# Sample states of a four-head recurrence made one head later, the last ones behind the next block's norm

## The chip, the cores and the metric

One core of a Trainium2 chip runs the whole program. The metric is the device time in microseconds (us) of one execution; the kernel before was timed three times. A profile is one further execution. The engines are TensorE (PE, matmuls; PEld its weight loads), VectorE (DVE), ScalarE (ACT), GpSimd (POOL) and SyncE (SP), which only issues DMAs here.

## The reference, cut to what matters

One decoder layer works on 2048 prompt tokens behind 16 learned meta tokens, and on 8 separate sample tokens that have states of their own. The part that the change touches is a gated recurrence with 4 heads and a 128x128 state for each head:

```python
f = lb + (1.0 - lb) * sigmoid(f_logit);  k = 1.0 - f
S_t = diag(f_t) S_{t-1} + k_t v_t^T       # one state per head; the prompt from zero, each sample from its own
o_t = S_t^T q_t
o = rms_norm_per_head(o) * norm_g * silu(g)
```

For the prompt this is computed in chunks of 64 tokens. A sample has a single step: read its state, multiply it by f, add the outer product of k and v, write it out (8 samples x 4 heads x 64 KB), and multiply it by q. A diagonal state-space mixer (S5), an output projection, a second RMSNorm and a gated convolutional FFN complete the layer.

## The kernel before

The prompt goes through in four blocks of 512 tokens (b = 0 to 3). Block 0 carries the 16 meta tokens and the 8 samples as 24 more columns. Every fp32 operand of a large matmul is split into two parts by ACT (`wh`, `ah`) and DVE (`wl`, `al`), and each product is made of three matmuls.

For each block the code first makes the normalised, transposed input (`norm1(b)`, through `norm_block`: L538 loads 128 rows, L530 squares them, L520 and L521 make the factor, L542 scales, L547 transposes, L86 multiplies by the gain, L552 and L83 split), then runs `head(b, a, h)` for the four heads, and then `u_proj(b, a)`, the input of the S5 mixer (matmuls L480, evictions L778). In block 0 the code of `s5_factors`, `s5_setup` and `s5_rotations` stands among this: it makes S5's tables and stores them in DRAM (`tab_d`).

In block 0, `head` has two parts. The prompt part makes f, k, the running products and q (L610 to L646), v and g (L500, L514), the chunk states and outputs (L690 to L714), the norm (L720 to L723) and the transposed result `mixh` (L726, L732). The sample part (L735 to L767) does, in this order: transpose k of the samples (L736, L738), spread v (L741), load the 8 states (L745) and multiply them by f on POOL (L746), make the outer products on PE (L749) and add them (L80), store the states (L751), make the meta tokens' scores (L753), multiply by q (L757, L758), normalise (L760 to L763) and write 10 columns of `mixh` (L765 to L767). It reads the prompt part's tiles `kd` (of `hk`) and `qd` (of `hP`), which have two buffers each, in L753.

Buffers set much of the order. The pool `x4p` has two buffers: each sample part takes both (`vb` for the spread v, `s0` for the states), and the row tiles of `norm1` take the same two. PSUM has three banks `mm` for the large matmuls, three banks `hg` for the heads, two banks `tp`. The scratch pool `nt` has four buffers, used by `norm_block` (`tm`) and by `u_proj` (`us`).

The order of instructions in each engine's queue is made by the framework's scheduler: what stands earlier in the code has priority, and later instructions fill in where the scheduler expects an engine to be free. Each queue then runs in its order. So table work of `s5_rotations` (L413 to L442) stands between instructions of heads 2 and 3 in the queues, though its code comes behind all four heads.

Of the kernel before, what the change touches and what calls it, by code (L numbers as in the profile page):

```python
# [9 lines left out]
F32 = mybir.dt.float32  # L10
# [12 lines left out]
W = META + BT + NS  # L23
PW = W
MT, SP = BT, BT + META
# [12 lines left out]
def kernel(  # L38
# [7 lines left out]
    nc = tc.nc  # L46
# [6 lines left out]
    sm = pool("sm", 4)  # L53
# [10 lines left out]
    exa = pha.enter_context(tc.tile_pool(name="exa", bufs=1))  # L64
# [29 lines left out]
    def gbank():  # L94
        return pg.tile([128, 512], F32, name="hg")
# [173 lines left out]
    E = {}  # L269
# [134 lines left out]
    def s5_rotations():  # L404

        rt = u_tile()
        mc, ms = v3(rt, 7, 32), v3(rt[:, 224:], 7, 32)
        t0, t1 = rt[:, 448:480], rt[:, 480:512]
        nc.vector.tensor_copy(mc[:, 0], sv[:, C4])
        nc.vector.tensor_copy(ms[:, 0], sv[:, S4])  # L410
        for i in range(1, 7):
            c, s_ = mc[:, i - 1], ms[:, i - 1]
            stt(ms[:, i], s_, 2.0, c, op0=OP.mult, op1=OP.mult)  # L413
            mul(t0, s_, s_)
            ts_(mc[:, i], t0, -2.0, 1.0, op0=OP.mult, op1=OP.add)
            unit(mc[:, i], ms[:, i], t0, t1)
        for q in range(4):
            tab = bigt()
            X, Y = v3(tab, 8, 129), v3(tab[:, 1032:], 8, 129)
            gs = slice(8 * q, 8 * q + 8)  # L420

            def mate(lo, n):
                ACT(Y[0:64, :, lo:lo + n], X[64:128, :, lo:lo + n], AF.Copy, scale=-1.0)
                ACT(Y[64:128, :, lo:lo + n], X[0:64, :, lo:lo + n], AF.Copy)

            nc.gpsimd.memset(X[0:64, :, 0:1], 1.0)
            nc.gpsimd.memset(X[64:128, :, 0:1], 0.0)
            nc.vector.tensor_copy(X[0:64, :, 1], sv[0:64, C4, gs])
            ts_(X[64:128, :, 1], sv[64:128, S4, gs], -1.0, None, op0=OP.mult)
            mate(0, 2)  # L430
            ta = rt[:, 512 + 512 * (q % 2):1024 + 512 * (q % 2)]
            for i in range(7):
                n = 1 << i
                tav = v3(ta, 8, n)
                X1 = X[:, :, n + 1:2 * n + 1]
                mul(X1, X[:, :, 1:n + 1], mc[:, i, gs, None].to_broadcast([128, 8, n]))
                mul(tav, Y[:, :, 1:n + 1], ms[:, i, gs, None].to_broadcast([128, 8, n]))
                sub(X1, X1, tav)
                mate(n + 1, n)
            for src, lo, hi in ((X, TC, TS), (Y, TS, TC)):  # L440
                for p, o in ((slice(0, 64), lo), (slice(64, 128), hi)):
                    dma(tab_d[2 * q:2 * q + 2, p].rearrange("b p x -> p b x")[:, :, o:o + 516],  # L442
                        src[p].rearrange("p (b g) j -> p b (g j)", b=2))
# [156 lines left out]


    def head(b, a, h):
        S = S_st[:, h, :]
        c0, c1 = 0, W if b == 0 else BT
        cols = ((0, 256), (256, W - 256)) if b == 0 else ((0, BT),)
# [28 lines left out]
        pq = fm_mm(wq, a, 8, cols)  # L634
# [3 lines left out]
        if b == 0:  # L638
            ksm = sm.tile([128, 8], F32, name="ksm", bufs=2)
            nc.vector.tensor_copy(ksm, kk[:, SP:W])  # L640
            qmd = E["qm"].rearrange("p a b -> p (a b)")[:, 32:32 + 41 * 7 + 1:41]
            nc.vector.tensor_copy(qmd, pq[1][0][:, SP - 256:W - 256])
        kd = kk
        mul(kd[:, c0:c1], ks, R[:, c0:c1])
        lead = lambda t: t[:, 0:BT].rearrange("p (c h s) -> p c h s", h=2, s=64)[:, :, 0, :]
# [17 lines left out]
        for t2_ in range(2):  # L663
            p = v3(bank(), 2, 256)
# [7 lines left out]
        if b == 0:  # L672
            pe = bank()
            ex_mm(pe[:, :256], wu, (4, 4), E["stat"], 104)
            t = ex_sum(pe, 40, 64, 256)
            ie = exa.tile([40, 256], F32, name="ie")
            add(ie, pe[:40, :256], t)
            ge = exa.tile([40, 128], F32, name="ge")
            ACT(ge, ie[:, 128:256], AF.Silu)

            nc.vector.tensor_scalar(kt[:, MT:SP], kd[:, MT:SP], pl[:, 8:9], None, op0=OP.mult)
            pm = gbank()
            nc.tensor.transpose(pm[:16, :128], kt[:, MT:SP], ident)
            ktm = exa.tile([16, 128], F32, name="ktm")
            nc.vector.tensor_copy(ktm, pm[:16, :128])
# [41 lines left out]
        if b % 2:  # L727
            mh = E["mxp"].tile([128, BT], F32, name="mixh", bufs=4)
        else:
            mh = hgp.tile([128, 10 + BT], F32, name="mixh", bufs=4)  # L730
        ng = vec[:, NG + h:NG + h + 1]
        ACT(mh[:, :BT], px.rearrange("p a b -> p (a b)"), AF.Copy, scale=ng)  # L732
        if b == 0:

            tp = gbank()  # L735
            nc.tensor.transpose(tp[:8, :128], ksm, ident)  # L736
            kts = exa.tile([40, 128], F32, name="kts")
            ACT(kts[32:40], tp[:8, :128], AF.Copy)  # L738
            vb = x4()
            vbd = v3(vb, 8, 128)[32:40]  # L740
            tt_(vbd, ie[32:40, None, 0:128].to_broadcast([8, 8, 128]),  # L741
                                    ident[32:40, 32:40, None].to_broadcast([8, 8, 128]), op=OP.mult)
            s0 = x4()
            s0v = v3(s0, 8, 128)
            dma_w(s0v, state_hgrn[0, :, h].rearrange("n k v -> k n v"))  # L745
            nc.gpsimd.tensor_tensor(s0v, s0v, fsm[:, :, None].to_broadcast([128, 8, 128]), op=OP.mult)  # L746
            for i in range(2):
                p = gbank()
                mm(p, kts[32:40], vb[32:40, 512 * i:512 * i + 512], start=True, stop=True)  # L749
                add(s0[:, 512 * i:512 * i + 512], s0[:, 512 * i:512 * i + 512], p)  # L750
            dma(hg_s[0, :, h].rearrange("n k v -> k n v"), s0v)  # L751
            pa = gbank()
            mm(pa[:16, :16], kd[:, MT:SP], qd[:, MT:SP], start=True, stop=True)  # L753
            nc.vector.copy_predicated(E["atte"][:, 0:16], mask[:16, :16], pa[:16, :16])
            po = gbank()
            for n in range(8):
                mm(po[:40, :128], E["qm"][:, n, :], s0v[:, n, :], start=(n == 0), stop=False)  # L757
            mm(po[:40, :128], E["atte"], ie[0:16, 0:128], start=False, stop=True)  # L758
            ss = sm.tile([128, 1], F32, name="ss", bufs=6)
            ACT(junk[:40, :128], po[:40, :128], AF.Square, accum_out=ss[:40])  # L760
            r = rstd_of(ss[:40], 1, 1.0 / 128)
            me = exa.tile([40, 128], F32, name="me")
            stt(me, po[:40, :128], r, ge, op0=OP.mult, op1=OP.mult)  # L763
            pm = gbank()
            nc.tensor.transpose(pm[:, :40], me, ident[:40, :40])  # L765
            ts_(mh[:, FM_:FS], pm[:, 14:16], ng, None, op0=OP.mult)
            ts_(mh[:, FS:FS + 8], pm[:, 32:40], ng, None, op0=OP.mult)  # L767
        return mh

    def u_proj(b, a):  # L770

# [237 lines left out]
    def norm1(b):  # L1009
        A[b] = new_act(b)  # L1010
        if b == 0:
            norm_block(None, NMIX, A[b], range(0, 2), x_first)
            ex_in(A[b])
            norm_block(None, NMIX, A[b], range(2, 4), x_first)
        else:
            norm_block(lambda t: x_prompt[0, b * BT + t * 128:b * BT + t * 128 + 128, :], NMIX, A[b])
# [7 lines left out]
    for b in range(NB):  # L1024
        MIX[b] = []
        last = b == NB - 1
        if b > 0:
            M[b - 1] = new_act(b - 1)
        for h in range(4):
            if last and h == 2:  # L1030
                U[b] = u_proj(b, A[b])
                fin = []
                stage_out(b - 1, lambda q: s5(b, U[b], None, (q,), fin))
                M[b] = new_act(b)
                for f in fin:
                    f(M[b])
            if last and h < 2:
                s5(b - 1, U[b - 1], M[b - 1], range(4 * h, 4 * h + 4))
            elif last:
                s5(b, U[b], M[b], (2 * h, 2 * h + 1))  # L1040
            elif b > 0:
                s5(b - 1, U[b - 1], M[b - 1], (2 * h, 2 * h + 1))
            MIX[b].append(head(b, A[b], h))
            if b == 0 and h == 0:
                s5_factors()
                setup = s5_setup()
                next(setup)
            if b == 0 and h == 1:
                next(setup, None)
        if last:  # L1050
            break
        if b == 0:
            s5_rotations()
            norm1(1)
        U[b] = u_proj(b, A[b])
        if b == 0:
            pha.close()
            E["mxp"] = pool1("mxp", 4)
        else:
            glu(b - 1, M[b - 1])  # L1060
            norm1(b + 1)
            mix_split(b - 1, M[b - 1], MIX[b - 1])
            out_proj(b - 1, M[b - 1])
# [221 lines left out]
```

## Time and profile before

| | us |
|---|---|
| timed runs: median (lowest, highest) | 2586.27 (2585.12, 2598.17) |
| profiled execution, its own time | 2598.71 |
| its span on the core | 2597.0 |
| PE busy in the span | 2475.8 (95%) |
| DVE busy | 1453.3 (56%) |
| ACT busy | 903.6 (35%) |
| POOL busy | 167.9 (6%) |

The profiled execution took 12.44 us (0.48%) more than the median of the timed ones. Busy time counts instructions, weight loads of PE apart; POOL's spans are rough. PEclk is the granted share of TensorE's full clock: 1.00 is 2.4 GHz and 0.5 is 1.2 GHz. A wait in brackets behind an instruction is the idle time of its engine before it and what ended it.

### The profile page before, as it was taken

Reading aid. Unit: us, or ns where it says so; the run is one execution under the profiler, and the core shown is the slowest. Engines: PE = TensorE matmul, PEld = TensorE weight load, DVE = VectorE, ACT = ScalarE, POOL = GpSimd, SP = SyncE. Lnnn points to the kernel's source line nnn. Section 1 sums busy time; section 2 is a strip of 40 time slices with the busy share of each in tenths; the row PEclk is TensorE's granted clock in tenths of the full one; section 3 lists DMA queues with packets and bytes.
Section 4 is the critical chain, followed back from the end, with each engine's and each line's share of the span. In section 5 each row is a group of like instructions: output and inputs, shape, how many; then the busy total and the mean of one; then the engine's idle time right before and its main releaser. Section 6 shows DMA issues by size and latency. Waiting matters only on the chain.

```text
span 2597.0 us, 35488 instructions
## 1 busy us (share of the span) xinstructions
PE 2475.8 (95%) x14315; PEld 2149.5 (83%) x14315; DVE 1453.3 (56%) x2954; ACT 903.6 (35%) x1552; POOL 167.9 (6%) x254
## 2 busy tenths in 40 slices
PE   7896998999998999999999999999999999999998
PEld 6785876898887888898988888889888888888886
DVE  6875688668668688564343433344843333333444
ACT  3544354434434445342322222223531313131222
POOL 2232100100000000100000000000310000000000
PEclk9897999999999999999999999999999999999999
DMA  4346433544464562642111111111441111111111
GB/s 128 101 126 190 110 104 130 140 152 139 123 189 144 160 221 88 228 124 65 49 49 44 47 49 41 49 41 50 156 130 49 49 49 49 49 49 49 41 53 77
DMA packets 263658, 252.22 MB, mean 97 GB/s; under 512 B 11367, under 2 KB 233471, under 8 KB 259390
## 3 DMA queue, kind: packets, MB, share of 16 engines
q1 hardware_dynamic: 253416, 220.42, 28.1%
q0 software_dynamic: 9904, 29.48, 3.5%
q8 instruction: 112, 1.84, 0.3%
q14 instruction: 52, 0.43, 0.1%
q10 hardware_dynamic: 174, 0.06, 0.0%
HBM read 216.41 MB, written 33.27 MB: 96 GB/s over the span
## 4 chain that ended last, share of the span: by engine, by line
PE 72%; DVE 10%; issue 4%; ACT 3%; DMA 3%; POOL 1%; SPq 0%; POOLq 0%; ACTq 0%; DVEq 0%
PE mm L480 42%; PE mm L1209 9%; PE hg L1209 9%; PE mm L500 7%; DVE hf L632 1%; PE mm L514 1%; DVE wl L83 1%; DVE sB L86 1%; POOL rstd L521 1%; DVE sA L885 1%; PE tp L899 1%; DMA st<-in_w_in_dram 1%; DVE sA L86 1%; PE tp L547 1%; PE tp L847 1%
## 5 line engine op out<-in xcount | busy, mean ns | idle before, releaser
L480 PE MATMUL mm<-ah,wh 128*128 128x512 f32 (+3 forms) x2320 | 819.8, 353 | 4.5 <-ACT ah L552 3.3
L480 PE MATMUL mm<-al,wh 128*128 128x512 f32 (+3 forms) x2320 | 816.6, 352 | 1.1 <-DVE al L83 1.1
L480 PE MATMUL mm<-ah,wl 128*128 128x512 f32 (+3 forms) x2320 | 816.5, 352 | 0.5 <-DVE wl L83 0.5
L449 ACT ACTIVATE wh<-st 128x1024 fp32r<-128x1024 f32 (+1 forms) x264 | 275.7, 1046 | 731.1 <-PE mm L480 317.2
L83 DVE TENSOR_TENSOR wl<-st,wh 128x1024 fp32r<-128x1024 f32 (+1 forms) x264 | 318.2, 1206 | 345.6 <-ACT wh L449 344.0
L480 PEld LDWEIGHTS mm<-ah,wh 128*128 128x128 f32 x2320 | 442.5, 191 | 60.3 <-ACT ah L552 3.9
L480 PEld LDWEIGHTS mm<-ah,wl 128*128 128x128 f32 x2320 | 442.1, 191 | 55.9 <-DVE wl L83 1.0
L480 PEld LDWEIGHTS mm<-al,wh 128*128 128x128 f32 x2320 | 442.2, 191 | 55.2 <-DVE al L83 1.6
L500 PE MATMUL mm<-wh,ah 128*128 128x256 f32 x1024 | 294.5, 289 | 8.3 <-ACT hg L671 3.2
L500 PE MATMUL mm<-wh,al 128*128 128x256 f32 x1024 | 293.5, 287 | 5.9 <-DVE al L83 5.0
L500 PE MATMUL mm<-wl,ah 128*128 128x256 f32 x1024 | 291.6, 286 | 1.1 <-DVE wl L83 1.1
L500 PEld LDWEIGHTS mm<-wh,ah 128*128 128x128 f32 x1024 | 197.5, 193 | 11.6 <-ACT hg L671 3.4
L500 PEld LDWEIGHTS mm<-wh,al 128*128 128x128 f32 x1024 | 198.0, 193 | 8.4 <-DVE al L83 6.2
L500 PEld LDWEIGHTS mm<-wl,ah 128*128 128x128 f32 x1024 | 197.5, 193 | 1.8 <-DVE wl L83 1.5
L86 DVE TENSOR_TENSOR c<-c,mm 128x512 f32<-128x512 f32 (+1 forms) x110 | 63.8, 580 | 211.8 <-PE mm L480 210.4
L1209 PE MATMUL mm<-wh,gh 128*128 128x512 f32 x352 | 137.5, 391 | 0.0
L1209 PE MATMUL hg<-wh,gl 128*128 128x512 f32 x352 | 137.2, 390 | 0.0
L1209 PE MATMUL hg<-wl,gh 128*128 128x512 f32 x352 | 137.2, 390 | 0.0
L1209 PE MATMUL mm<-wh,gl 128*128 128x512 f32 x352 | 137.2, 390 | 0.0
L1209 PE MATMUL mm<-wl,gh 128*128 128x512 f32 x352 | 137.2, 390 | 0.0
L1209 PE MATMUL hg<-wh,gh 128*128 128x512 f32 x352 | 137.1, 389 | 0.0
L80 DVE TENSOR_TENSOR hacc<-hacc,hg 128x512 f32<-128x512 f32 x96 | 65.8, 686 | 88.2 <-PE hg L1209 87.7
(384 smaller groups left out, 3050.4 us busy)
## 6 DMA issues: line engine op xcount, KB each, us to landing
st<-in_ffn_w_up_dram SPq DMA_DIRECT2D x96, 512.0 KB
big<-tab_d SPq DMA_DIRECT2D x32, 1156.0 KB
st<-in_w_in_dram SPq DMA_DIRECT2D x48, 512.0 KB
st<-in_ffn_w_down_dram SPq DMA_DIRECT2D x40, 512.0 KB
st<-in_w_in_dram SPq DMA_DIRECT2D x64, 256.0 KB
st<-in_w_out_dram SPq DMA_DIRECT2D x32, 512.0 KB
x<-in_x_prompt_dram SPq DMA_DIRECT2D x30, 512.0 KB
h_d<-x POOLq DMA_DIRECT2D x16, 512.0 KB, 5.1
```

The lines of the kernel that those rows point to most:

```text
L80: tt_(o, a, b, op=OP.add)
L83: tt_(o, a, b, op=OP.subtract)
L86: tt_(o, a, b, op=OP.mult)
L449: ACT(hi[:, :n], st[:, :n], AF.Copy)
L480: mm(p[:, :n], w[wi][:, k, :], a[ai][:, k, c0:c0 + n], start=(i == 0), stop=(i == 3 * nk - 1))
L500: o = mm(dst, lhs(ai, k), (hi, lo)[wi][:, kk, :], start=(i == 0), stop=(i == tot - 1))
L514: mm(dst[:m], stat[:, k, :m], w[:, kk, :], start=(i == 0), stop=(i == tot - 1))
L521: nc.gpsimd.tensor_tensor(r, r, mhalf[:ss.shape[0], :n], op=OP.pow)
L547: nc.tensor.transpose(p[:, k, :], x[:, kk * 128:kk * 128 + 128], ident)
L632: nc.vector.reciprocal(R[:, c0:c1], P[:, c0:c1])
L847: mm(pes[i // ng][:, i % ng, :], Bk[:, i, :], UT[:, i // 2, :nj], start=True, stop=True)
L1209: mm(ps_[t], gs[b, f0 + k][ai][:, t * 128:t * 128 + 128], wus[i][wi][:, kk, :], start=(k == 0 and j == 0), stop=(k == nf - 1 and j == 2))
```

## The change

`head` becomes a generator. In block 0 it stops behind the prompt part (`yield`); the loop then lets the sample part of the head before it run, so that in the code the order is: prompt 0, prompt 1, sample 0, prompt 2, sample 1, prompt 3, sample 2, `norm1(1)`, sample 3, `s5_rotations`, `u_proj(0)`. Before, it was prompt 0, sample 0, ..., prompt 3, sample 3, `s5_rotations`, `norm1(1)`, `u_proj(0)`. What a sample part needs later gets a place that lasts: q of the samples is copied into a small tile `qsm` and from there into `qm` when the sample part runs, and `ie` and `ge` get two buffers.

```diff
@@ head
         if b == 0:
             ksm = sm.tile([128, 8], F32, name="ksm", bufs=2)
             nc.vector.tensor_copy(ksm, kk[:, SP:W])
-            qmd = E["qm"].rearrange("p a b -> p (a b)")[:, 32:32 + 41 * 7 + 1:41]
-            nc.vector.tensor_copy(qmd, pq[1][0][:, SP - 256:W - 256])
+            qsm = sm.tile([128, 8], F32, name="qsm", bufs=2)
+            nc.vector.tensor_copy(qsm, pq[1][0][:, SP - 256:W - 256])
...
-            ie = exa.tile([40, 256], F32, name="ie")
+            ie = exa.tile([40, 256], F32, name="ie", bufs=2)
...
-            ge = exa.tile([40, 128], F32, name="ge")
+            ge = exa.tile([40, 128], F32, name="ge", bufs=2)
...
         ACT(mh[:, :BT], px.rearrange("p a b -> p (a b)"), AF.Copy, scale=ng)
-        if b == 0:
+        MIX[b].append(mh)
+        if b == 0:
+            yield
+            qmd = E["qm"].rearrange("p a b -> p (a b)")[:, 32:32 + 41 * 7 + 1:41]
+            nc.vector.tensor_copy(qmd, qsm)
             tp = gbank()
...
-        return mh
@@ the loop over the heads
-            MIX[b].append(head(b, A[b], h))
+            hd = head(b, A[b], h)
+            if b == 0:
+                next(hd)
+                if h:
+                    next(samples, None)
+                samples = hd
+            else:
+                for _ in hd:
+                    pass
...
         if b == 0:
+            norm1(1)
+            next(samples, None)
             s5_rotations()
-            norm1(1)
         U[b] = u_proj(b, A[b])
```

## Rows read from the trace of the kernel before

**Rows 1.** The page: the span, PE's busy time, the granted clock in 40 slices.

```profile
span 2597.0 us, 35488 instructions
...
PE 2475.8 (95%) x14315; PEld 2149.5 (83%) x14315; DVE 1453.3 (56%) x2954; ACT 903.6 (35%) x1552; POOL 167.9 (6%) x254
...
PEclk9897999999999999999999999999999999999999
```

**Rows 2.** Busy time by stretch: from:to, length, busy by engine, PEclk, DMA share, GB/s.

```profile
71.00:80.00 9.00, 8.55 (x42) 5.68 (x41) 5.97 (x35) 2.95 (x7) 1.62 (x2) 0.81 0.20 58
121.00:130.00 9.00, 7.78 (x38) 5.20 (x38) 8.49 (x27) 2.16 (x4) 4.40 (x7) 0.81 0.72 186
...
165.00:176.00 11.00, 11.00 (x42) 6.73 (x41) 6.72 (x16) 5.13 (x12) 2.54 (x3) 0.61 0.26 72
...
213.00:226.00 13.00, 12.03 (x54) 7.71 (x54) 7.75 (x22) 5.07 (x15) 2.96 (x5) 0.74 0.83 251
226.00:250.00 24.00, 8.55 (x36) 6.68 (x35) 13.46 (x25) 10.03 (x20) 5.45 (x10) 0.56 0.55 188
250.00:272.00 22.00, 22.00 (x147) 20.99 (x146) 5.25 (x13) 5.87 (x10) 4.34 (x8) 0.94 0.47 148
```

**Rows 3.** Waits of PE from 40 to 270 us: total, times, longest.

```profile
PE tp L547 <- DVE x L542: 7.5, 1, 7.5
PE tp L547 <- DVE rstd L520: 6.9, 1, 6.9
...
PE mm L714 <- DVE Sp L710: 1.4, 1, 1.4
```

**Rows 4.** The chain of work that ended last, from 218 us: start, us, what.

```profile
218.52 0.69 DVE x L80
...
219.78 7.42 DMA out_dram<-x
...
227.28 4.35 DMA x<-in_x_prompt_dram
...
235.72 5.89 DMA x<-in_x_prompt_dram
...
249.44 27.53 PE mm L480 x168
```

**Rows 5.** The eviction line of u_proj, 200 to 272 us: durations, first and last start.

```profile
L778 ACT ACTIVATE nt<-mm x8: 363/370/384, 249.0 to 267.0; 128x256 f32<-128x256 f32 x8
```

**Rows 6.** PE in order of time, around the sample parts of heads 1 to 3.

```profile
122.22 0.30 PE L726 MATMUL hg<-ident,hg 128*128 128x128 f32 x1 [1.27 <-DVE hg L723]
...
123.37 1.98 PE L749 MATMUL hg<-x,kts 8*128 8x512 f32 x4
125.28 0.22 PE L753 MATMUL hg<-hP,hk 128*16 128x16 f32 x2
...
126.10 3.38 PE L757 MATMUL hg<-x,qm 128*40 128x128 f32 x16
129.40 0.59 PE L758 MATMUL hg<-ie,atte 16*40 16x128 f32 x2
...
164.76 0.33 PE L726 MATMUL hg<-ident,hg 128*128 128x128 f32 x1 [1.52 <-DVE hg L723]
...
200.05 1.16 PE L701 MATMUL hg<-hv,hf 128*128 128x128 f32 x8 [3.04 <-ACT hf L698]
```

**Rows 7.** DVE in order of time: head 2 takes its k tile.

```profile
126.08 0.42 DVE L615 TENSOR_SCALAR hk<-hf 128x536 f32<-128x536 f32 x1
```

**Rows 8.** SP's queue in order of time: the state load of head 3.

```profile
198.99 0.51 SPq L745 DMA_DIRECT2D x<-in_state_hgrn_dram  x1
```

**Rows 9.** POOL and DVE in order of time: the multiplication by f, and DVE beside it.

```profile
204.37 1.95 POOL L746 TENSOR_TENSOR x<-x,fsm 128x1024 f32<-128x1024 f32 x1 [4.48 <-DMA x<-in_state_hgrn_dram]
...
204.68 2.19 DVE L83 TENSOR_TENSOR big<-big,U 128x512 f32<-128x512 f32 x1
...
226.25 0.69 DVE L83 TENSOR_TENSOR big<-big,U 128x512 f32<-128x512 f32 x1
```

## The prediction

> **What bounds the kernel now.** I read the page first: PE is busy for 95% of the span, and its granted clock is full almost everywhere except in the first slices [rows 1]. So a change pays only where PE waits or runs at a low clock, and all of this change lies in the first tenth of the span. I then cut that tenth into stretches. Two things stand out [rows 2]. From 226 to 250 us PE is busy for 8.55 of 24 us. And in the four stretches that hold the sample parts (from 71, 121, 165 and 213 us) the mean granted clock is 0.81, 0.81, 0.61 and 0.74, a mixture of the 2.4 and 1.2 GHz levels. In the third of them PE was busy without a pause, but with the sample part's small matmuls, and it had waited for head 2's own norm just before (the 1.52 us ahead of 164.76 [rows 6]).
>
> The list of PE's waits names the two large ones [rows 3]: both stand before the transposes of `norm1(1)`, 7.5 and 6.9 us. The chain of work says what they hang on [rows 4]: the last addition to head 3's new states (218.52), the store of these states (7.42 us), which must end before their buffer is free, the load of a row tile into that buffer (4.35 us), its norm, a second load (5.89 us), its norm, and only then the matmuls of `u_proj` go on at 249.44. These matmuls themselves need nothing of the norm. They stand still because their banks are not emptied: the first eviction of `u_proj` starts at 249.0 [rows 5], though the three banks were filled well before. In the code `u_proj` draws its scratch tiles behind those of `norm1(1)`, out of the same four buffers, so its evictions wait for that norm. From the last addition of head 3's sample part to the first eviction it is 249.0 − 218.5 = 30.5 us, most of it three transfers and work on one tile at a time.
>
> **The change part by part.** Nothing leaves the program. Added are four copies `qsm` to `qm` of 128x8 elements on DVE. DVE is busy for 5.25 to 13.5 us in each of the six stretches, in only one of which it is near full [rows 2], so they cost nothing; without that cover they cost less than 1.7 us, since an instruction on 128x536 elements takes 0.42 us [rows 7]. All else is order.
>
> *The norm of block 1.* Its row tiles now take the two buffers behind head 2's sample part and not behind head 3's. The chain of 30.5 us stays; its start moves. The question is when the last addition of head 2's sample part comes, now that head 3's prompt part goes ahead of it. In head 3's prompt part PE is nearly full until it waits 3.04 us ahead of 200.05 [rows 6], so from 197.0. There the sample part finds room. Its outer products take 1.98 us on PE in head 1 [rows 6] and an addition 0.69 us [rows 4], with the other addition beside the products: I put the last addition at 201. Then the first eviction of `u_proj` comes at 201 + 30.5 = 231.5, 17.5 us earlier. But the sample part of head 3, which now lies ahead of the eviction, will lie behind the norm. On PE such a part takes 1.98 + 0.22 + 3.38 + 0.59 = 6.2 us [rows 6]. The gain is 17.5 − 6.2 = 11.3 us. While the chain runs, PE has head 2's sample part, the rest of head 3, 32 transposes and three banks of `u_proj` to do, as it had before. Bounds: if the addition comes at 212.3 or later, nothing is won (218.5 − 212.3 − 6.2 = 0); if it slips between the prompt matmuls before 195, the gain ends where PE has no wait left, 7.5 + 6.9 + 3.0 = 17.4 us [rows 3, 6].
>
> The DMAs move with it: the four row loads, one state load and one store. On SP's queue the row loads are moved ahead of head 3's state load; behind it wait the weights of `u_proj`, which have two staging buffers to run ahead in. On POOL's queue the stores of the S5 tables come later. What is late next is the S5 tables and head 3's 10 sample columns. The tables are first read when S5 starts on block 0, and the chain shows 27.5 us of other matmuls behind the norm, of `u_proj` and the next head [rows 4]; the columns are read later still. So I cost both at nothing; if the tables' cover were gone, every us that they end late would be one us.
>
> *The ends of the heads.* At the end of a prompt part PE waits for the norm of the head: 1.27 us in head 1 and 1.52 us in head 2 [rows 6], and 1.4 us for a scaled state [rows 3], 4.2 us in all. (Head 0 has no sample part to fill with, and head 3 is in the first term.) With a finished head's sample matmuls at hand these can be filled: all of it, or nothing, since the scheduler puts instructions where it expects the gap. I take half, 2.1 us.
>
> *The clock.* What the low clock takes in a stretch is at most (1 − clock) x length: 0.19 x 9 twice, 0.39 x 11, 0.26 x 13, and 0.06 x 22 behind the long wait [rows 2], so 1.7 + 1.7 + 4.3 + 3.4 + 1.3 = 12.4 us. Some will come back, when the small matmuls lie between large ones and waits shrink. But the small matmuls stay, and in the third stretch the clock fell though PE never paused. Between 0 and 12.4 I take a third, 4.1 us, nearest to the stretches that follow a wait (3.4 + 1.3).
>
> *POOL beside DVE.* The four multiplications by f move to other moments. One of them shows a price [rows 9]: a 128x512 subtraction on DVE that began within it took 2.19 us where the same took 0.69 us alone, 1.5 us more. By the Trainium skill (SBUF — State Buffer, "Who interferes with whom") a VectorE instruction with two SBUF inputs and a GpSimd instruction that reads SBUF share one read port, and the one that starts second is blocked until the other ends. The row agrees with it. The multiplications can now fall among a prompt part's DVE work as before: I take 0, between −1.5 (that one gone) and 4 x 1.5 = +6.0 us.
>
> Sum: 11.3 + 2.1 + 4.1 = 17.5 us off. The profiled execution has a span of 2597.0 us and a time of 2598.71 us, 1.71 us around it, which would become 2581.2. The median of the timed runs is 12.4 us lower than that execution. Nothing in the first tenth says that its waits belong to this execution alone, so I take the same 17.5 us off the median: 2586.27 − 17.5 = 2568.8 us. Behind 272 us PE is the bound up to the end, so what is won stays won.
>
> **The rivals.**
>
> *The chain starts no earlier.* Head 2's sample part gets its states late, its addition comes at 212 or behind, and the norm waits as before. For it: everything of head 3's prompt part goes first, PE's first wait there is at 197, and the outer products need banks that the head's own end uses too. Against it: 15 us lie between 197 and 212. Only the small terms are left, 0 to 6.2 us: about 2583 us.
>
> *The order does not change.* The queues are already filled across parts, so the scheduler may place the sample parts where they were. Against it: the row tiles' buffers are drawn in the new order in any case. 2586 us.
>
> *The lock of POOL and DVE is paid in each head.* All four multiplications fall beside DVE work on the prompt's path, 6.0 us: 2568.8 + 6.0 = 2574.8 us. For it speaks the price at 204.68 [rows 9], against it that the instruction held up there worked on an S5 table, off the prompt's path. This is what the Trainium skill's rule (SBUF — State Buffer, "Who interferes with whom") would do at its worst.
>
> *Slower: the prompt parts wait for two-buffered tiles.* L753 of head h reads its `hk` and `hP`, and head h + 2 needs these buffers at L615. Now head 0's sample part lies behind prompt part 1. Where head 1's L753 stands today it ends at 125.50, and head 2's L615 starts at 126.08 [rows 6, 7]: 0.6 us free. If L753 is queued behind outer products whose bank waits for a state load, it slips by load and multiplication (204.37 − 198.99 = 5.4, and 1.95 [rows 8, 9]) and two additions (1.38): 8.7 us, in heads 2 and 3, so 17.4 us with no gain from the norm: 2603.7 us. It decides as soon as L753 ends behind the moment at which head h + 2 wants L615; from 14 us in all it makes the kernel slower by more than it can be measured. Against it: a state load can be issued a whole head ahead.
>
> **How the numbers follow.** Forecast 0.50; chain no earlier 0.25; order unchanged 0.07; the lock 0.08; slower 0.10. Half a per cent, 12.9 us, is about what tells a change from none here: faster means under 2573.3, slower over 2599.2. Of the forecast 0.48 lies below 2573.3, and of the lock half: faster 0.52. Slower is the last rival, 0.10. The rest is 0.38. The forecast's own range is 2551 (17.4 + 4.2 + 12.4 + 1.5 = 35.5 us off) to 2575 (the first term alone). For 8 in 10 I take 2556 to 2590: it holds the forecast but for its lowest end, the lock and both cases without effect with some scatter, and leaves out the slower one.
>
> **What would show it.** Right: the two waits of the norm's transposes gone or below 5 us together; row loads of `norm1(1)` issued before 212 us; the first eviction of `u_proj` near 231 us; granted clock over 0.8 in the sample parts' stretches. Wrong: the row loads still behind 215 us; a new wait of PE on head 3's state load between `u_proj`'s matmuls; L615 of heads 2 or 3 waiting for PE's L753; or S5 on block 0 waiting for its tables.

## The result and the profile after

| | before | after | ratio (95% interval) |
|---|---|---|---|
| timed on one chip, median of 11 runs each, us | 2591.07 | 2605.08 | 1.0053 [1.0038, 1.0069] |
| profiled execution, us | 2598.71 | 2609.07 | |
| its span, us | 2597.0 | 2607.4 | |

The change made the kernel slower by half a per cent, some 14 us, where 17.5 us less were forecast. The interval lies above 1, so this is no scatter. (The prediction started from 2586.27 us, the median of three runs of the kernel before; over 11 runs it is 2591.07 us.)

The page after: the span, and PE's busy time, which rose by 8.1 us although the program has the same 14315 matmuls [rows 1].

```profile
span 2607.4 us, 35487 instructions
...
PE 2483.9 (95%) x14315; PEld 2145.9 (82%) x14315; DVE 1455.7 (56%) x2958; ACT 903.6 (35%) x1552; POOL 167.2 (6%) x254
```

The same stretches as [rows 2], after.

```profile
71.00:80.00 9.00, 9.00 (x75) 8.85 (x74) 8.76 (x51) 3.81 (x7) 0.00 (x0) 1.00 0.20 58
121.00:130.00 9.00, 9.00 (x59) 6.58 (x58) 7.89 (x20) 1.90 (x6) 2.02 (x3) 1.00 0.57 134
165.00:176.00 11.00, 10.82 (x63) 8.09 (x64) 7.88 (x20) 4.67 (x10) 4.02 (x6) 0.84 0.43 115
213.00:226.00 13.00, 10.74 (x58) 7.73 (x57) 8.12 (x24) 4.93 (x14) 2.15 (x3) 0.84 0.79 245
226.00:250.00 24.00, 13.66 (x46) 9.11 (x45) 15.17 (x27) 10.46 (x19) 7.00 (x11) 0.50 0.66 197
250.00:272.00 22.00, 22.00 (x149) 20.51 (x149) 6.27 (x15) 5.13 (x10) 6.26 (x9) 0.94 0.55 164
```

In the first four stretches the granted clock rose to 1.00, 1.00, 0.84 and 0.84. In the hole from 226 to 250 us PE is busy for 13.66 us instead of 8.55, but at the lower level, 1.2 GHz (0.50). The next two fences are the answers to [rows 3] and [rows 5]: PE's longest waits from 40 to 270 us, and the first eviction of `u_proj` with the row loads of `norm1(1)` from 200 us on.

```profile
PE tp L547 <- DVE x L542: 9.1, 3, 6.6
PE hg L702 <- ACT hf L699: 7.4, 3, 4.2
PE mm L715 <- DVE Sp L711: 5.9, 1, 5.9
PE hg L727 <- DVE hg L724: 4.2, 3, 1.8
PE hg L754 <- DVE x L746: 3.2, 1, 3.2
```

```profile
L782 ACT ACTIVATE nt<-mm x8: 362/367/385, 240.6 to 268.4; 128x256 f32<-128x256 f32 x8
...
L538 SPq DMA_DIRECT2D x<-in_x_prompt_dram x6: 328/328/347, 215.3 to 259.7; - x6
```

The two waits of the norm, 14.4 us, became 9.1 us, and other waits came: 5.9 us at L715 (1.4 us before, there L714), 7.4 us at L702 (4.8 us before, there L701). The one at L715 belongs to this execution: two experiments below have the same queues, and there it is 1.6 us (e7) and not in the list (e2). The eviction starts 8.4 us earlier. The next fence shows DVE and SP in order of time: head 2's two additions and the loads around them.

```profile
213.84 0.69 DVE L80 TENSOR_TENSOR x<-x,hg 128x512 f32<-128x512 f32 x1
215.27 0.69 DVE L80 TENSOR_TENSOR x<-x,hg 128x512 f32<-128x512 f32 x1 [0.74 <-PE hg L754]
...
171.26 0.37 SPq L750 DMA_DIRECT2D x<-in_state_hgrn_dram  x1
...
215.26 0.35 SPq L538 DMA_DIRECT2D x<-in_x_prompt_dram  x1
```

Head 2's states were loaded from 171.26 us on, yet their last addition comes at 215.27 and not at 201; the first row load goes out with it.

**Where the time went.** I numbered the matmuls of both traces and compared their starts. At number 1500 (271 us) after is 1.4 us behind, at number 7000 (1132 us) 3.0 us ahead; from there it falls back steadily, to 10.6 us behind at the end. Nearly all of that loss lies in one line, the FFN's down-projection (L1209 before, L1222 after), which the diff doesn't touch. Its last 144 matmuls, first before and then after, as grouped rows: durations in ns (min/median/max), then first and last start in us.

```profile
L1209 PE MATMUL mm<-wh,gh x24: 388/389/481, 2553.7 to 2583.7; 128*128 128x512 f32 x24
...
L1209 PE MATMUL hg<-wl,gh x24: 388/389/390, 2556.3 to 2586.2; 128*128 128x512 f32 x24
```

```profile
L1222 PE MATMUL mm<-wh,gh x24: 394/394/483, 2563.3 to 2594.2; 128*128 128x512 f32 x24
...
L1222 PE MATMUL hg<-wl,gh x24: 394/394/397, 2566.0 to 2596.8; 128*128 128x512 f32 x24
```

From the first to the last start it is 2586.2 − 2553.7 = 32.5 us before and 2596.8 − 2563.3 = 33.5 us after, 227 and 234 ns for each of 143 steps, with PE busy and its clock at 1.00 in both. The line has 2112 matmuls in 32 such stretches; their 2080 steps take 472.6 us before and 486.0 us after: 13.4 us, nearly the whole slowdown.

The first 1160 us need a caution. The next fence has this line's first group in three profiles: before, after, and the first experiment, whose instruction queues are those of before.

```profile
L1209 PE MATMUL mm<-wh,gh x352: 387/389/481, 1194.1 to 2583.7; 128*128 128x512 f32 x176
```

```profile
L1222 PE MATMUL mm<-wh,gh x352: 388/394/483, 1191.1 to 2594.2; 128*128 128x512 f32 x176
```

```profile
L1209 PE MATMUL mm<-wh,gh x352: 388/394/483, 1182.7 to 2585.6; 128*128 128x512 f32 x176
```

With the same queues the first start is 1194.1 us in one execution and 1182.7 us in another. So a difference of a few us ahead of the FFN can't be read from one profile of each, and the experiments go by medians. Matmul 1500 shows the same: it starts at 270.9, 266.0, 270.4, 269.2 and 270.7 us in five profiles with the queues of before (before, e1, e4, e5, e6), and at 272.4, 265.7 and 267.5 us in three with those of after (after, e2, e7). By these profiles the new order neither won nor lost anything that could be told.

### The profile page after: what moved, and what is told of

Its sections match the earlier page's. It is cut to its first block, busy times and chain, and to the rows that moved or that the text cites. A ratio compares the mean times of both kernels' runs of the same rounds, so it can differ in the third digit from the quotient of the medians.

```text
span 2607.4 us, 35487 instructions
## 1 busy us (share of the span) xinstructions
PE 2483.9 (95%) x14315; PEld 2145.9 (82%) x14315; DVE 1455.7 (56%) x2958; ACT 903.6 (35%) x1552; POOL 167.2 (6%) x254
## 4 chain that ended last, share of the span: by engine, by line
PE 76%; DVE 12%; ACT 5%; DMA 3%; issue 2%; POOL 1%; SPq 0%; ACTq 0%; POOLq 0%; DVEq 0%
PE mm L480 43%; PE mm L1222 9%; PE hg L1222 9%; PE mm L500 7%; DMA st<-in_w_in_dram 2%; DVE wl L83 1%; DVE hf L633 1%; PE mm L514 1%; DVE sB L86 1%; POOL rstd L521 1%; DMA st<-in_w_out_dram 1%; DVE sA L889 1%; PE tp L903 1%; ACT wh L449 1%; DVE sA L86 1%
## 5 line engine op out<-in xcount | busy, mean ns | idle before, releaser
L83 DVE TENSOR_TENSOR wl<-st,wh 128x1024 fp32r<-128x1024 f32 (+1 forms) x264 | 317.9, 1205 | 347.6 <-ACT wh L449 346.3
L500 PE MATMUL mm<-wh,ah 128*128 128x256 f32 x1024 | 292.4, 287 | 5.7 <-ACT wh L449 2.8
L500 PE MATMUL mm<-wh,al 128*128 128x256 f32 x1024 | 291.7, 285 | 5.9 <-DVE al L83 5.0
L500 PE MATMUL mm<-wl,ah 128*128 128x256 f32 x1024 | 289.6, 284 | 1.1 <-DVE wl L83 1.1
L500 PEld LDWEIGHTS mm<-wh,al 128*128 128x128 f32 x1024 | 195.6, 191 | 8.4 <-DVE al L83 6.2
L500 PEld LDWEIGHTS mm<-wh,ah 128*128 128x128 f32 x1024 | 195.2, 191 | 9.0 <-ACT wh L449 3.2
L500 PEld LDWEIGHTS mm<-wl,ah 128*128 128x128 f32 x1024 | 195.2, 191 | 1.8 <-DVE wl L83 1.5
L1222 PE MATMUL mm<-wh,gh 128*128 128x512 f32 x352 | 139.4, 396 | 0.0
L1222 PE MATMUL hg<-wh,gl 128*128 128x512 f32 x352 | 139.3, 396 | 0.0
L1222 PE MATMUL hg<-wl,gh 128*128 128x512 f32 x352 | 139.3, 396 | 0.0
L1222 PE MATMUL mm<-wl,gh 128*128 128x512 f32 x352 | 139.3, 396 | 0.0
L1222 PE MATMUL mm<-wh,gl 128*128 128x512 f32 x352 | 139.2, 396 | 0.0
L1222 PE MATMUL hg<-wh,gh 128*128 128x512 f32 x352 | 139.2, 395 | 0.0
L80 DVE TENSOR_TENSOR hacc<-hacc,hg 128x512 f32<-128x512 f32 x96 | 65.9, 687 | 93.6 <-PE hg L1222 91.6
```

Source lines behind the costliest of these rows:

```text
L80: tt_(o, a, b, op=OP.add)
L83: tt_(o, a, b, op=OP.subtract)
L500: o = mm(dst, lhs(ai, k), (hi, lo)[wi][:, kk, :], start=(i == 0), stop=(i == tot - 1))
L1222: mm(ps_[t], gs[b, f0 + k][ai][:, t * 128:t * 128 + 128], wus[i][wi][:, kk, :], start=(k == 0 and j == 0), stop=(k == nf - 1 and j == 2))
```

## The experiments

Two questions: why does the down-projection run slower, and what did the new order itself do? "Aligned" below means that no tile of the later stages moves.

### Why the down-projection runs slower

The addresses of the compiled program differ in one respect that reaches the later stages. `qsm` (two buffers of 32 bytes) was put into the pool `sm`, and every tile that lies behind this pool in SBUF moved up by 64 bytes. Among them are `gh` and `gl`, the stationary operands of L1209 (from 144000 to 144064); the moving operands `wh` and `wl` (from 30080 on) stayed.

**e1_before_64**: before, with 64 unused bytes at the same place.

```diff
-        drow = sm.tile([32, 16], F32, name="drow", bufs=1)
+        drow = sm.tile([32, 32], F32, name="drow", bufs=1)[:, :16]
```

> The kernel before with one small tile (drow) made 64 bytes longer per partition, so that every tile allocated behind it, gh and gl of the FFN among them, lies 64 bytes further on; no instruction and no queue's order differs. Theory 'place': the down-projection's 2112 matmuls start 0.2335 us apart and not 0.227, 13.6 us in all: ratio to the kernel before about 1.005. Theory 'order' (the loss comes from the new order of the head's parts): ratio 1.000, matmuls 0.227 us apart.

**e2_after_128**: the same edit on the changed kernel, so that its tiles lie 128 bytes further than before.

> The changed kernel with the same 64 bytes more, so that gh and gl lie 128 bytes further on than in the kernel before; the queues' order is that of the changed kernel. Theory 'place' with a grain of 128 bytes: down-projection matmuls 0.227 us apart again, some 13.6 us less than the changed kernel; what is left is what the new order does, about 3 us less than before by the count of matmuls at 1160 us: ratio to the kernel before about 0.999. Theory 'order': ratio stays at 1.005. If any shift costs (no grain of 128 bytes): 0.2335 us and 1.005 too, and the sweep of places tells these two apart.

**e4_sweep**: before, with the buffers of `gh` and `gl` 2080 bytes apart, so that they lie at mixed places.

```diff
-                    hi = gp.tile([128, BT], F32R, name=f"gh{b % 2}")
-                    lo = gp.tile([128, BT], F32R, name=f"gl{b % 2}")
+                    hi = gp.tile([128, BT + 8], F32R, name=f"gh{b % 2}")[:, :BT]
+                    lo = gp.tile([128, BT + 8], F32R, name=f"gl{b % 2}")[:, :BT]
```

> The kernel before with gh and gl 32 bytes longer per buffer, so that their four buffers start at 0, 32, 64 and 96 bytes behind a multiple of 128; order as before. Theory 'place': groups of down-projection matmuls whose stationary tile starts at 64 run at 0.2335 us from start to start, those at 0 at 0.227; the trace shows what 32 and 96 do. Theory 'order': all at 0.227.

**e5_before_256**: before, with `drow` 256 bytes longer (`[32, 80]` in place of `[32, 16]`).

> The kernel before with the small tile 256 bytes longer, so that gh and gl lie 256 bytes further on and the split weights wh and wl where they were; order as before. Theory 'relation' (what counts is whether the stationary tile gh, gl and the moving tile wh, wl start at the same place within 256 bytes, as they do in the kernel before): down-projection matmuls 0.227 us apart. Rival 'any move' or a longer grain: 0.232 to 0.234 us, as with 64 and 128 bytes.

**e6_before_both64**: before, with 64 unused bytes in the pool ahead of all of them, so that moving and stationary operands move up together.

```diff
-    zero = cst.tile([128, 1], F32, name="zero")
+    zero = cst.tile([128, 17], F32, name="zero")[:, :1]
```

> The kernel before with a tile at the head of memory made longer, so that wh, wl, ah, al, gh and gl all lie 64 bytes further on; order as before. Theory 'relation': the distance of the operands is as before, so 0.227 us. Rival 'absolute place' (gh, gl must start at 128 within 256 whatever wh does): 0.2335 us, and perhaps the up-projection slower too, which the other shifts left at 0.2267.

**e7_after_0**: the changed kernel, with `qsm` in a pool behind which nothing moves. Its queues are those of the changed kernel.

```diff
-            qsm = sm.tile([128, 8], F32, name="qsm", bufs=2)
+            qsm = exa.tile([128, 8], F32, name="qsm", bufs=2)
```

> The changed kernel with qsm in the pool exa, so that gh, gl and all other tiles behind the pool sm lie where they lay in the kernel before; queues as in the changed kernel. Theory 'place': down-projection at 0.227 us, and the time is what the new order alone does: within 4 us of the kernel before, ratio 0.9985 to 1.0015. Theory 'order': ratio 1.004 to 1.005, as the changed kernel.

Measured (the pace is the mean step from one L1209 or L1222 matmul to the next, where they follow without a pause; the place is the distance between stationary and moving operand, modulo 256 bytes, against that of before):

| kernel | order | place | pace, ns | median us (runs) | ratio |
|---|---|---|---|---|---|
| before | before | 0 | 227.2 | 2591.07 (11) | 1 |
| after | after | 64 | 233.7 | 2605.08 (11) | 1.0053 [1.0038, 1.0069] |
| e1_before_64 | before | 64 | 233.7 | 2605.83 (9) | 1.0044 [1.0026, 1.0061] |
| e2_after_128 | after | 128 | 232.8 | 2603.70 (10) | 1.0041 [1.0027, 1.0054] |
| e4_sweep | before | mixed | 232.3 | 2601.83 (1) | one run |
| e5_before_256 | before | 0 | 227.2 | 2590.38 (1) | one run |
| e6_before_both64 | before | 0 | 227.2 | 2593.37 (1) | one run |
| e7_after_0 | after | 0 | 227.2 | 2594.00 (12) | 1.0000 [0.9989, 1.0010] |

The rows of e1, then those of e6:

```profile
L1209 PE MATMUL mm<-wh,gh x24: 394/394/483, 2554.8 to 2585.6; 128*128 128x512 f32 x24
...
L1209 PE MATMUL hg<-wl,gh x24: 394/394/397, 2557.4 to 2588.2; 128*128 128x512 f32 x24
```

```profile
L1209 PE MATMUL mm<-wh,gh x24: 389/389/486, 2548.3 to 2578.4; 128*128 128x512 f32 x24
...
L1209 PE MATMUL hg<-wl,gh x24: 388/389/389, 2550.9 to 2580.9; 128*128 128x512 f32 x24
```

e1 settles the cause: the old order with 64 empty bytes pays the same, and e7 gives it all back with the new order. It is not the place of `gh` by itself (e6 moves it by the same 64 bytes and keeps the pace) but its place against tiles that e1 left where they were. The moving operands `wh` and `wl` are among these, and the matmuls of this line read nothing else of them; that it is these two and no other tile of that group is argued and not shown. A grain of 128 bytes fell with e2, one of 256 stands with e5. e4 didn't tell single distances apart: sorted by distance, in steps of 32 bytes, the mean steps lie between 230.8 and 232.9 ns, and the 347 at distance 0 took 232.3 ns too. So the distance of a matmul's own two operands doesn't set its step by itself. What makes PE slower, no run here shows.

### What the order did

**e3_after_128_tp** and **e8_after_0_tp**: as e2 and e7, with the five PSUM tiles of the sample part out of the banks `tp` instead of `hg` (the first is shown).

```diff
-            tp = gbank()
+            tp = tbank()
```

> As the run before, and the five PSUM tiles of the sample part are taken from the two banks tp and not from the three banks hg. Theory 'banks': the sample part of head h could not start before the next head's prompt part had ended, since it draws hg banks behind that part; with tp banks head 2's second addition (215.3 us in the changed kernel) comes before 195 us, block 1's rows are loaded before 205 us, the waits ahead of the norm's transposes (9.1 us) mostly go, and the kernel is 8 to 17 us faster than the run before, ratio about 0.993 to the kernel before. Rival 'queue': the sample part is late because the scheduler prefers every prompt instruction; then its additions stay at 210 us or later and the time is that of the run before within 3 us.

> As the run before, and the sample part's five PSUM tiles come from the banks tp. The first eviction of u_proj comes near 232 us (232.6 with tp banks in the run with 128 bytes), but the heads' ends and the S5 tables take it back: ratio to the kernel before 0.998 to 1.001. If the earlier norm were worth what the prediction gave it, 0.994.

e3 gave 2602.42 us, ratio 1.0044 [1.0028, 1.0060], at the place 128; e8, aligned, 2592.32 us, ratio 1.0000 [0.9990, 1.0010]. DVE in order of time, then the eviction line, of e3:

```profile
204.68 0.69 DVE L80 TENSOR_TENSOR x<-x,tp 128x512 f32<-128x512 f32 x1 [0.77 <-PE tp L754]
```

```profile
L782 ACT ACTIVATE nt<-mm x8: 364/384/385, 232.6 to 260.2; 128x256 f32<-128x256 f32 x8
```

The same addition in e2 and in e7, whose queues are those of after:

```profile
209.44 0.69 DVE L80 TENSOR_TENSOR x<-x,hg 128x512 f32<-128x512 f32 x1 [1.55 <-PE hg L754]
```

```profile
210.85 0.69 DVE L80 TENSOR_TENSOR x<-x,hg 128x512 f32<-128x512 f32 x1 [1.20 <-PE hg L754]
```

The banks hold the sample part back in the order: head 2's first outer product is PE's matmul 1249 with the banks `hg`, right behind head 3's first transposes (1246), and matmul 1185 with the banks `tp`, ahead of them (1235). In time this is worth less than the 10.6 us between after (215.3) and e3 (204.7), for the three profiles with the changed queues give 215.3, 209.4 and 210.9 us, and e8 gives 209.7. Pair by pair it is 4.8 us (e2 and e3) and 1.2 us (e7 and e8). The eviction of e3 lies 1.1 us from the 231.5 of the prediction; that is luck, since e8 has it at 237.7 us. And the median doesn't fall, where e3 expected 8 to 17 us. One profile of each shows where what is won goes. In head 1 PE now waits 6.4 us at L684 for DVE, and from matmul 1600 to 2000 it takes 7.6 us longer than before in both, where e7 takes as long as before. The wait of e8:

```profile
102.03 0.38 PE L684 MATMUL hg<-ident,hf 128*16 128x128 f32 x1 [6.42 <-DVE hf L682]
```

Three kernels then turned the last head alone.

**e9_last_head_only**: before, where only head 3 stops behind its prompt part, and the norm goes between.

```diff
...
-            MIX[b].append(head(b, A[b], h))
+            hd = head(b, A[b], h)
+            next(hd, None)
+            if not (b == 0 and h == 3):
+                next(hd, None)
...
-            s5_rotations()
             norm1(1)
+            next(hd, None)
+            s5_rotations()
```

> The order before, with one exception: in the last head of block 0 the norm of block 1 stands between the prompt part and the sample part, and s5_rotations behind the sample part; heads 0 to 2 are as before, there is no qsm, and no tile moves. The row tiles' buffers are free from the store of head 2's sample part on, near 177 us, so the row loads can be issued some 40 us earlier than at 218.5 us and nothing of the norm hangs on a sample part. Theory 'an earlier norm pays': the waits of 7.5 and 6.9 us ahead of the norm's transposes go, head 3's sample part (6.2 us of PE) lies among u_proj's matmuls, and 6 to 14 us stay won to the end: ratio 0.995 to 0.998. Theory 'won time is given back', as in the kernel with the tp banks: the first eviction of u_proj comes over 10 us earlier than 249.0, but other waits (tables, heads of block 1) take it back: ratio 0.999 to 1.001.

**e10_last_head_rot_first**: as e9, with the last two lines exchanged.

> As the run before, with s5_rotations ahead of head 3's sample part. Theory 'the tables are what takes it back': with the tables made earlier the time is at least 2 us below that of the run before (ratio lower by 0.001 or more), and the tables' loads come near 219 to 235 us as in the kernel before. Theory 'the tables cost nothing': the same ratio as the run before within 0.001.

**e11_norm_first_only**: before, with the norm ahead of the rotations and no sample part moved.

```diff
-            s5_rotations()
             norm1(1)
+            s5_rotations()
```

> The kernel before with norm1(1) ahead of s5_rotations in the code and nothing else moved; head 3's sample part still goes first and holds the row tiles' buffers. Theory 'the chain hangs on head 3's sample part': the first eviction of u_proj stays within 4 us of 249.0 and the ratio is 0.999 to 1.001. Theory 'the chain is slowed by the table work on DVE and ACT between its links': the eviction comes 5 us or more earlier and the ratio is 0.998 or less.

e9: 2581.18 us, ratio 0.9957 [0.9941, 0.9972]. e10: 2582.62 us, 0.9947 [0.9928, 0.9966]. e11: 2593.06 us, 0.9990 [0.9978, 1.0003]. So an earlier norm pays, 11 us (0.0043 x 2592), and stays paid: in e9's profile PE is 15.1 us ahead of before at matmul 1500 and 20.6 us at the end. (Some of that is the profile of before: e5, with the same queues, is 1.8 and 8.3 us ahead of it.) Between e9 and e10 nothing can be told, so no effect of the tables' order is seen. In e11 the eviction starts at 247.8 us: the chain does hang on the sample part. The eviction line of e9, then of e11:

```profile
L778 ACT ACTIVATE nt<-mm x8: 365/372/385, 230.7 to 253.1; 128x256 f32<-128x256 f32 x8
```

```profile
L778 ACT ACTIVATE nt<-mm x8: 365/372/385, 247.8 to 266.5; 128x256 f32<-128x256 f32 x8
```

The rest asks why the change, aligned, wins nothing where e9 wins half a per cent. All are aligned, made from e7.

**e12_norm_before_two**: the norm also ahead of head 2's sample part.

```diff
                 next(hd)
+                if h == 3:
+                    norm1(1)
                 if h:
                     next(samples, None)
...
-            norm1(1)
             next(samples, None)
```

> The changed kernel with qsm where it moves no tile (as in the run with qsm in the pool exa), and with the norm of block 1 ahead of the sample parts of heads 2 and 3, not only of head 3. Samples 0 and 1 stay one head late, now nothing of the norm hangs on the sample part of head 2: the row tiles take the buffers behind head 1's sample part. Theory 'the delay itself is harmless, what takes the gain is the norm hanging on a sample part that has just been put off': first eviction of u_proj before 235 us and ratio 0.994 to 0.998, as in the kernel in which only the last head is reordered. Theory 'putting off the sample parts costs as much as the norm wins' (the prompt parts end later, the outer products of two heads meet behind the norm): ratio 0.999 to 1.001, with the eviction early or not.

**e13_delay_0_1**: heads 0 and 1 put off, head 2 whole, head 3 as in e9.

```diff
-                if h:
+                if 0 < h < 3:
                     next(samples, None)
+                if h == 2:
+                    next(hd, None)
```

> Order: prompt 0, prompt 1, sample 0, prompt 2, sample 1, sample 2, prompt 3, norm of block 1, sample 3; qsm where it moves no tile. So the last head is as in the order that wins, and the sample parts of heads 0 and 1 are put off by one head as in the change. Theory 'putting off heads 0 and 1 costs by itself': the gain of the last head is mostly lost, ratio 0.998 to 1.001. Theory 'it costs nothing; what costs is a second sample part behind the norm': ratio 0.994 to 0.997.

**e14_delay_2**: heads 0 and 1 whole; norm ahead of the sample parts of heads 2 and 3.

```diff
-                if h:
+                if h < 2:
+                    next(hd, None)
+                if h == 3:
+                    norm1(1)
                     next(samples, None)
...
-            norm1(1)
             next(samples, None)
```

> Order: heads 0 and 1 whole as in the kernel before, then prompt 2, prompt 3, norm of block 1, sample 2, sample 3; qsm where it moves no tile. Theory 'putting off heads 0 and 1 costs by itself': without that the norm's gain stays, ratio 0.994 to 0.997. Theory 'a second sample part behind the norm costs the gain' (another 6.2 us of TensorE's work that no longer fills the waits ahead of the norm): ratio 0.998 to 1.001.

**e15_delay_0_1_only**: as e13, with head 3 whole, and rotations and norm as in before.

```diff
-                if h == 2:
+                if h >= 2:
                     next(hd, None)
...
-            norm1(1)
-            next(samples, None)
             s5_rotations()
+            norm1(1)
```

> Order: prompt 0, prompt 1, sample 0, prompt 2, sample 1, sample 2, prompt 3, sample 3, s5_rotations, norm of block 1; qsm where it moves no tile. Only the sample parts of heads 0 and 1 are put off. Theory 'putting them off costs by itself': slower than before, ratio 1.002 to 1.004 (the 0.25% and 0.40% lost beside the norm). Theory 'the delay costs only through the norm, by holding its buffers longer': ratio 0.999 to 1.001.

**e16_delay_0_only**: as e15, with head 0 alone put off (the conditions are `h == 1` and `h >= 1`).

> As the run before, with only the sample part of head 0 put off. Theory 'each delayed part costs': about half of the run before, ratio 1.001 to 1.002. Theory 'no cost of its own': 0.999 to 1.001. A ratio below 0.999 would say that head 0's delay pays (in the profiles with it TensorE is some 2 us ahead in the first two heads).

| kernel | put off | norm of block 1 ahead of the sample part of | median us | ratio |
|---|---|---|---|---|
| e7_after_0 | 0, 1, 2 | 3 | 2594.00 | 1.0000 [0.9989, 1.0010] |
| e9_last_head_only | none | 3 | 2581.18 | 0.9957 [0.9941, 0.9972] |
| e14_delay_2 | 2 | 2 and 3 | 2580.87 | 0.9953 [0.9937, 0.9969] |
| e13_delay_0_1 | 0, 1 | 3 | 2587.81 | 0.9982 [0.9970, 0.9995] |
| e12_norm_before_two | 0, 1, 2 | 2 and 3 | 2585.45 | 0.9993 [0.9983, 1.0004] |
| e15_delay_0_1_only | 0, 1 | none | 2595.76 | 1.0022 [1.0011, 1.0033] |
| e16_delay_0_only | 0 | none | 2597.39 | 1.0025 [1.0013, 1.0037] |

(Medians of different rows come from different chips. The ratio compares with the kernel before on the same chip; the plain quotient of the two medians differs from it by up to 0.0014.) Putting off the sample parts of heads 0 and 1 costs by itself: 0.0022 x 2592 = 5.7 us in e15, and as much with head 0 alone, so e16's first theory, half of it, fell. The parts add up: e9 with e15 gives 0.9979, e13 measured 0.9982. A second sample part behind the norm shows no cost (e14 against e9). e7 lies 0.0018 above e13, some 5 us; they differ in the place of head 2's sample part, which in e7 goes behind head 3's prompt part and ahead of the norm. That it costs by making the norm late is not shown: e12 frees the norm of it and starts the eviction at 223.0 us, e7 at 236.1, and yet e12 can't be told from e7. e14 with e15 gives 0.9975 for e12, with both intervals up to 0.9994; e12 measured 0.9993, so the sum isn't contradicted there, nor borne out.

Where the delay costs stays open. One candidate shows in single profiles. ACT, DVE and PE of e15 in order of time, then the same split on DVE in before and in e7:

```profile
110.37 1.06 ACT L449 ACTIVATE wh<-st 128x1024 fp32r<-128x1024 f32 x1 [8.13 <-DMA st<-in_w_in_dram]
...
111.45 1.22 DVE L83 TENSOR_TENSOR wl<-st,wh 128x1024 fp32r<-128x1024 f32 x1 [5.71 <-ACT wh L449]
...
113.32 0.79 PE L715 MATMUL mm<-Sp,hP 128*128 128x128 f32 x2 [5.28 <-DVE Sp L711]
```

```profile
118.67 1.23 DVE L83 TENSOR_TENSOR wl<-st,wh 128x1024 fp32r<-128x1024 f32 x1 [0.98 <-ACT wh L449]
```

```profile
110.32 1.23 DVE L83 TENSOR_TENSOR wl<-st,wh 128x1024 fp32r<-128x1024 f32 x1 [2.03 <-ACT wh L449]
```

Head 1's prompt part gets ahead of its weights. The split of a weight tile (`wl`, L83) stands on DVE's queue between the links of the chunk states (L711, L80); it waits 5.71 us for ACT, which waits for the weight's DMA, and PE waits 5.28 us for the state behind it. Before, the same split waits 0.98 us, past the states. But with heads 0 and 1 put off, the wait of the split is 6.34 us in after, 0 in e2 and 2.03 us in e7, which have the same queues, and 1.74 us in e12, 1.15 us in e13 and 5.71 us in e15. So it changes from one execution to the next, and one profile can't price it. e13 and e16 (1.99 us) pay by their medians though their profiles hardly show it.

## Why the prediction was wrong

**The step that failed first** is the one on the copies `qsm`: the prediction costed them by the cover on DVE alone ("so they cost nothing"). As instructions they cost nothing. Their tile cost 13.4 us, by moving the operands of another stage. The sum had no term for a tile's place, and no stretch behind 272 us was looked at for it. "What is won stays won" holds for waits (e9 keeps its lead); "PE is the bound up to the end" was right, and just therefore a slower PE there counts in full. With the tile where it moves nothing (e7, 1.0000) the forecast of 17.5 us less fails too, by the following steps.

**The norm's chain (11.3 us).** That the first eviction hangs on a sample part's last addition and the norm behind it was right (e11, e9). The step that failed is "I put the last addition at 201": it came at 215.3, 209.4 and 210.9 us in the three profiles with these queues. That PE has room at 197 doesn't help, since the sample part draws its banks behind the whole prompt part of head 3; this was the point noted for the first rival, and with its own banks the outer products go ahead of that part's end (e3, e8). By the prediction's own bound, 218.5 − 212.3 − 6.2 = 0, nothing is won: the mean is 211.9 us, against 216.9 us for head 3's in the five profiles with the queues of before, and 5.0 − 6.2 is below 0. By an order in which the norm hangs on no late sample part e9 wins 11 us. That this is so near to 11.3 is in part luck: in e9 the first row load goes out at 166.9 us, and the chain is another than the one of 30.5 us from 201 on.

**The ends of the heads (2.1 us off)** had the wrong sign in all. The waits at the heads' norm did fall, from 6.3 us at L726 to 4.2 us at L727 (4.8 us in e2 and e7). But by the medians putting off heads 0 and 1 costs some 6 us (e15, e16). The term counted the waits that were to be filled and put what the delay costs at nothing, without a reason; where it costs stays open.

**The clock (4.1 us off).** In the first four stretches the loss by (1 − clock) x length fell from 11.1 to 0 + 0 + 1.8 + 2.1 = 3.9 us. But the low clock went where the waits went: over 40 to 290 us the mean granted clock was 0.88 before and 0.89 after. Fixed stretches were the wrong measure for work that moves.

**POOL beside DVE (0)** was not isolated by any run.

**The rivals.** "The chain starts no earlier" describes the order best, and e7 (1.0000) fits the lower end of its 0 to 6.2 us. The slower rival did not happen: L758, the former L753, started at 124.29 us and L616 took `hk` at 125.08 us without a wait. The kernel is slower by a mechanism that no rival had. In ratios: place 0.0053 (after against e7), delay of heads 0 and 1 0.0022, norm −0.0043, and 0.0018 with the late sample part of head 2. The last is itself e7 less e13, so only the two before it are checked by a run: they sum to −0.0021, and e13 measured −0.0018.

**The better kernel.** e9, e10 and e14 beat both, by 0.4 to 0.5%: leave the heads whole and let only the norm of the next block go ahead of the last sample parts.

## What to carry to other kernels

A new tile, however small, moves the tiles behind it in SBUF: compare the addresses of matmul operands of all later stages before and after, and put the tile where none moves. Work that is put off takes its place in a queue as its banks and buffers come free in the order of the code, and not as its engine has room. Before a wait in one profile is taken for the work of a change, look for it in a second profile with the same queues. To shorten a chain, take its cause out of the way (here the norm ahead of the sample part) rather than move everything one step.

## What was not expected of the hardware

The pace of 128x512 fp32r matmuls that follow without a pause, at full clock, changed with the distance between the addresses of the stationary and the moving operand: 227.2 ns where it was that of before modulo 256 bytes for the whole line (before, e5, e6, e7), 233.7 ns with 64 bytes more (after, e1), 232.8 ns with 128 more (e2), 232.3 ns on the mean of mixed places (e4). A rule for a single matmul doesn't follow, by e4. With 256 columns no loss was seen: L500's stationary slices lie at mixed places in block 0, and the median step is 118 ns there and 120 ns in the later blocks.
